# One tile and one transfer for four pairs of heads, and another layout for stored queries, keys and projection operands

## Chip, cores and metric

The kernel runs on 1 core of one Trainium2 chip. The metric is the device time of one execution in microseconds (us), taken as the median of several executions. The engines are TensorE (PE, with its weight loads PEld), VectorE (DVE), ScalarE (ACT), GpSimd (POOL) and SyncE (SP), whose queue issues nearly all transfers (DMAs).

## The reference, cut to what matters

One layer of a hybrid backbone over 1,024 latent tokens and 256 context tokens, width 1,024, fp32. One input projection feeds 8 heads of differential attention and 16 recurrent heads (RWKV-7, width 64, forwards and backwards); both outputs are gated and go through one output projection.

```python
u = h @ lp['w_in']
q, k, v, g_a, u_b, g_b = jnp.split(u, [...], axis=-1)
...
s = jnp.einsum('bqhmd,bkhmd->bhmqk', qblk, k).astype(F32) * scale   # m: the two halves of a head
p = jax.nn.softmax(s, axis=-1)
a = p[:, :, 0] - lam * p[:, :, 1]
...
sa = jnp.einsum('bhvk,bhk->bhv', S, -kk_t)                          # one recurrent step
S = S * w_t[:, :, None, :] + sa[..., None] * b_t[:, :, None, :] + v_t[..., None] * k_t[:, :, None, :]
y = jnp.einsum('bhvk,bhk->bhv', S, r_t)
...
x = x + gate[:, None, :] * (jnp.concatenate([o_a, o_b], axis=-1) @ lp['w_out'])
```

## The kernel before, in words

The program has two stages. All instructions are written out, and a scheduler puts them in order per engine by its own model and by priorities; each engine then runs its instructions strictly in that order.

**First stage** (`chunk`, `plan`, the generators `b_*`): for 66 blocks of 128 columns of `w_in`, three products of 24 matmuls each (`psg`, four PSUM banks) over 512, 512 and 256 tokens. A generator of each block does the rest between the products of later blocks. Weights `w` have one buffer and are loaded one block ahead; ACT casts them to `whi`, DVE and POOL make `wlo`. `b_k` prepares the recurrence of one pair of heads: `operands` and `gram` make the tiles `ra` (two buffers), `bk` and `km` (one each) for 8 chunks of 32 tokens and store them to the DRAM scratch `ra`, `kt` and `bt`. `b_qk` rotates a head's queries or keys (`suq`, `suk` are copies with swapped rows, made by DMA) and splits them into a high part `hi` and a low part. For the first six heads the high part goes in pieces of 512, 512 and 256 tokens through one buffer (tag `hi`, L624 to L627): ACT casts a piece, DVE subtracts, SP stores it, and the next cast writes the same buffer. Cached keys go through it too (`ko`, `ch`, L598 to L609), and their low part is `ck`. The low part of a whole head is one store (L628). For the last two heads the high part is one tile and one store. Scratch `qhi`, `qlo`, `khi`, `klo` has rows of 128 per head, so each store is `128 x n`.

**Second stage** (`mix_phase`): 10 items (2 groups of four pairs x 5 segments of 256 tokens), 4 parts per item, 2 steps per part, 80 steps in sequence. A step works for four pairs; these stand in two duos `w`, each with its own tiles `L` and `R` (two slots each, for even and odd parts). `step` multiplies `R` by `L` three times: L933 (into `bank[0]`, copied back into `R` by ACT, L940), L951 (into `bank[1]`, multiplied by the decay into the next `R` by DVE, L962) and L975 (the output `y`). `prep` (L812) multiplies `Bt` by the inverse `Tb` for one duo of the next part at the end of each step, and `put` (L818) copies that into `L`. `load_part` (L770 to L786) loads `L` from `kt` and `ra` and `R` from `vb`; `load_early` (L792 to L803) loads `Bt` and `Tb`. `inverse` makes the 32x32 inverses on POOL, in the layout `td0`. Between a step's pieces `fill` issues attention (`load_q`, `load_k`, `scores` L1099, `values` L1144), layer norms and the output projection (`project`, operand tile `of` from the scratch `oT`), each in its own order.

Of the kernel before, what the change touches and what calls it, by code (L numbers as in the profile page):

```python
# [10 lines left out]
F32 = mybir.dt.float32  # L11
# [7 lines left out]
P = 128  # L19
# [64 lines left out]
def tile_kernel(ctx: ExitStack, tc: tile.TileContext, i: dict, o: dict, heads=H, phases=3):  # L84
# [15 lines left out]
    scratch("ra", [H // 2, 5, NF, HD, 2, 2, 2, HN * HD])  # L100
    scratch("kt", [H // 2, 5, NF, CH, 2, 2, 2, HN * P])
    scratch("bt", [H // 2, 5, NF, 2, 2, CH, 2, HN * P])
# [21 lines left out]
    with ExitStack() as p1:  # L124
# [321 lines left out]
        def gram(p, d, it, c0, ra, bk):  # L446
# [13 lines left out]
            for h in range(2):  # L460
                nc.sync.dma_start(s["kt"][p // 2, it, :, :, p % 2, h, d].rearrange("f r y -> r f y"),
                                  km[64 * h:64 * h + CH].rearrange("r (f c) x -> r f (c x)", f=NF))
                nc.sync.dma_start(s["bt"][p // 2, it, :, h, d, :, p % 2].rearrange("f r y -> r f y"),
                                  km[64 * h + CH:64 * h + 64].rearrange("r (f c) x -> r f (c x)", f=NF))

        def operands(p, d, r, k, kn, wx, td, ta, c0):
# [12 lines left out]
            for h in range(2):  # L479
                nc.sync.dma_start(s["ra"][p // 2, it, :, :, p % 2, h, d].rearrange("f r y -> r f y"),  # L480
                                  ra[64 * h:64 * h + 64].rearrange("r (f c) x -> r f (c x)", f=NF))
# [96 lines left out]
        def b_qk(which, h):  # L578
            rows = slice(h * P, (h + 1) * P)
# [13 lines left out]
            if which == "k":  # L593
# [14 lines left out]
                nc.sync.dma_start(s["khi"][rows, 0:PAST], ch)  # L608
                nc.sync.dma_start(s["klo"][rows, 0:PAST], cv)  # L609
# [3 lines left out]
            if h >= heads - 2:  # L613
# [6 lines left out]
                spill(s[which + "hi"][rows, off:off + T], hi)  # L620
                spill(s[which + "lo"][rows, off:off + T], u[:, 0:T])
                return
            for n0, n in CHUNKS:
# [3 lines left out]
                spill(s[which + "hi"][rows, off + n0:off + n0 + n], hi)  # L627
            spill(s[which + "lo"][rows, off:off + T], u[:, 0:T])  # L628
# [96 lines left out]
def inverse(nc, s, td, rows, aw, tt, tmp):  # L725
    n = 32 * len(rows)
    for g, (p, sg) in enumerate(rows):
        bt = s["bt"][p // 2, sg + 1, :, :, :, :, p % 2].rearrange("f h d t y -> (f h d) t y")
        for c in range(HN):
            nc.sync.dma_start(aw[32 * g + c:32 * g + 32:HN], bt[:, :, c * P + 96:c * P + P])  # L730
# [14 lines left out]
def mix_phase(ctx, tc, i, o, s, ident, nhalf, dram, td0, neglam, subg, lnh, heads, psm):  # L745
# [8 lines left out]
    for w in duos:  # L754
        for n in range(2):
            L = cp.tile([P, 2, 2, 2, HN, P], F32, name=f"L{w}{n}")
            R = cp.tile([P, HN, 2, 2, P], F32, name=f"R{w}{n}")
            for e in range(2):
                for h in range(2):
                    for d in range(2):  # L760
                        nc.vector.tensor_copy(L[0:64, e, h, d, :, 0:64],
                                              ident[0:64, 0:64].unsqueeze(1).broadcast_to([HD, HN, HD]))
            slots[w, n] = (L, R)

# [5 lines left out]
    def load_part(j):  # L770
        m, f = j // NF, j % NF
        p0, sg = items[m]
        for w in duos:
# [4 lines left out]
        for w in duos:  # L778
            p = p0 + 2 * w
            L, R = slots[w, j % 2]  # L780
            for d in range(2):
                t0 = tok0(sg, d) + CH * HN * (NF - 1 - f if d else f)
                src = s["vb"][t0:t0 + CH * HN, p * P:(p + 2) * P].rearrange("(c t) y -> t c y", t=CH)
                nc.sync.dma_start(R[64:96, :, d].rearrange("t c e v -> t c (e v)"), src[:, ::-1] if d else src)
            nc.sync.dma_start(L[0:64, :, :, :, :, 64:128].rearrange("r e h d c y -> r e (h d c) y"),
                              s["ra"][p // 2, sg + 1, f].rearrange("r e h d (c y) -> r (e h d c) y", y=HD))  # L786
# [5 lines left out]
    def load_early(j, w):  # L792
        m, f = j // NF, j % NF
        p0, sg = items[m]
        p = p0 + 2 * w
        Bt = cp.tile([P, 2, HN, P], F32, tag=f"Bt{w}", name=f"Bt{j}_{w}")
        nc.sync.dma_start(Bt.rearrange("r e c y -> r (e c y)"),
                          s["bt"][p // 2, sg + 1, f].rearrange("h d r e y -> (h d) r (e y)"))
        Tb = cp.tile([P, 2, HN, CH], F32, tag=f"Tb{w}", name=f"Tb{j}_{w}")
# [3 lines left out]
        early[j, w] = (Bt, Tb)  # L803

    def prep(j, w, pp, chain):
        Bt, Tb = early.pop((j, w))
        for e in range(2):
            for c in range(HN):
                for q in range(4):
                    n = 96 * (HN * e + c)  # L810
                    g = slice(32 * q, 32 * q + 32)
                    follow(nc.tensor.matmul(pp[g, n:n + 96], Tb[g, e, c, :], Bt[g, e, c, 0:96], start=True, stop=True,  # L812
                                            tile_position=(32 * q, 32 * q)), chain)

    def put(j, w, pp):
        L = slots[w, j % 2][0]
        for q in range(4):
            nc.scalar.copy(L[96:128, :, q // 2, q % 2, :, 0:96],  # L818
# [7 lines left out]
    for w in duos:  # L826
        load_early(0, w)
# [8 lines left out]
    for w in duos:  # L836
        load_early(1, w)
# [44 lines left out]
    def start_item(w, m):  # L882
        p0, sg = items[m]
        R = slots[w, 0][1]
# [725 lines left out]
```

## Time and profile before

| | us |
|---|---|
| median of 3 runs | 2551.7 (2549.16 to 2551.72) |
| profiled execution, its own time | 2542.46 |
| its span, first to last instruction | 2540.3 |
| PE busy | 2299.6 (91%) |
| DVE / ACT / POOL busy | 1491.8 / 1222.8 / 1149.4 |
| mean granted clock of PE | 0.954 of full |

A line of the chain of waits gives the start and the time of a piece of work that the end of the program waited for; a DMA there counts from its issue to its landing. A line of the order in time gives start, busy time, engine and line, output and input, and in brackets how long the engine was idle before and what ended that. A DMA's own line (SPq) is only its issue.

### The profile page before, as it was taken

What the parts mean: (1) busy time and instruction counts of PE and PEld (TensorE: products, weight loads), DVE (VectorE), ACT (ScalarE), POOL (GpSimd) and SP (SyncE); (2) the same over time, 40 slices, a digit from 0 to 9 for tenths busy, and PEclk for the clock granted to TensorE, in tenths of its full rate; (3) what the DMA queues carried; (4) which work ended last, traced back from release to release, by engine and by line L of the source; (5) the groups of instructions that cost most, each with busy time, mean ns of one, the idle gap of its engine ahead of it and who ended that gap; (6) DMA issues with size and microseconds to landing.
All of it is one profiled execution on the core that took longest, in us unless ns stands there. A gap on an engine that the chain in (4) does not pass through costs nothing.

```text
span 2540.3 us, 60748 instructions
## 1 busy us (share of the span) xinstructions
PE 2299.6 (91%) x23907; PEld 1880.0 (74%) x23907; DVE 1491.8 (59%) x2950; ACT 1222.8 (48%) x2528; POOL 1149.4 (45%) x1665
## 2 busy tenths in 40 slices
PE   5999999999999999999578887999898889897886
PEld 4888888888888888887467676767686677675675
DVE  5665574646555755433347675666665564666676
ACT  3333444343433444332366676667566565553353
POOL 4244244352433443447554764457485121133274
PEclk9999999999999999999689898999999899998998
DMA  7455656566655565665998897786879889767435
GB/s 246 111 153 135 185 146 171 142 167 164 156 138 160 144 162 138 163 168 158 240 183 166 188 188 167 160 181 148 191 176 224 221 205 223 178 182 217 141 122 183
DMA packets 544893, 437.59 MB, mean 172 GB/s; under 512 B 182151, under 2 KB 481331, under 8 KB 542048
## 3 DMA queue, kind: packets, MB, share of 16 engines
q1 hardware_dynamic: 542512, 427.96, 66.8%
q0 software_dynamic: 2096, 5.75, 1.2%
q8 instruction: 189, 3.10, 0.5%
q14 instruction: 96, 0.79, 0.1%
HBM read 258.69 MB, written 163.86 MB: 166 GB/s over the span
## 4 chain that ended last, share of the span: by engine, by line
PE 53%; DMA 14%; POOL 9%; DVE 8%; SPq 6%; ACT 5%; issue 4%; POOLq 0%; DVEq 0%; ACTq 0%
PE sc L1099 4%; PE po L1144 4%; PE pg L452 3%; PE bank L951 3%; PE pa L1129 2%; PE yb L812 2%; DMA yn<-y 1%; PE pso L1352 1%; PE ptk L456 1%; PE bank L975 1%; PE bank L933 1%; PE psg_v L338 1%; ACT pb L1107 1%; PE psg_v L339 1%; PE psg_v L337 1%
## 5 line engine op out<-in xcount | busy, mean ns | idle before, releaser
L1099 PE MATMUL sc<-ka,q 128*128 128x512 f32 (+1 forms) x832 | 296.0, 447 | 40.1 <-DVE pb L1102 34.3
L1107 ACT ACTIVATE pb<-pb,mn 128x1536 f32<-128x1536 f32 (+1 forms) x160 | 218.3, 1365 | 97.8 <-DVE pb L1102 94.7
L1102 DVE TENSOR_SCALAR_CACHE_REDUCE pb<-sc,mn 128x512 f32<-128x512 f32 x256 | 191.5, 748 | 113.1 <-PE sc L1099 104.8
L1144 PE MATMUL po<-vk,aT 128*128 128x128 f32 x1600 | 233.6, 287 | 3.7 <-ACT aT L1131 3.6
L1144 PEld LDWEIGHTS po<-vk,aT 128*128 128x128 f32 x1600 | 212.9, 198 | 22.7 <-ACT aT L1131 5.7
L484 POOL TENSOR_SCALAR ta<-ta,ka 128x256 f32<-128x256 f32 x80 | 93.8, 1172 | 291.3 <-DVE bk L482 287.0
L738 POOL TENSOR_TENSOR tmp<-aw,tt 128x31 f32<-128x31 f32 (+15 forms) x310 | 165.5, 534 | 120.3 <-DMA aw<-bt 40.0
L459 ACT COPY km<-ptk 64x256 f32<-64x256 f32 x320 | 117.6, 367 | 209.5 <-PE ptk L456 169.8
L1099 PEld LDWEIGHTS sc<-ka,q 128*128 128x128 f32 x832 | 142.1, 202 | 81.7 <-DVE pb L1102 53.1
L740 POOL TENSOR_TENSOR tt<-tt,tmp 128x31 f32<-128x31 f32 (+15 forms) x310 | 183.3, 591 | 19.9
L962 DVE TENSOR_TENSOR R<-bank,wc 64x256 f32<-64x256 f32 x312 | 131.0, 420 | 76.4 <-PE bank L951 73.0
L818 ACT COPY L<-yb 32x384 f32<-32x384 f32 x312 | 146.6, 470 | 56.6 <-PE yb L812 52.8
L453 DVE TENSOR_TENSOR km<-pg,msk 128x512 f32<-128x512 f32 x80 | 55.2, 690 | 200.2 <-PE pg L452 188.4
L1121 DVE SCALAR_TENSOR_TENSOR pb<-pb,cc,pb 128x512 f32<-128x512 f32 (+1 forms) x208 | 170.6, 867 | 2.0
L1102 DVE TENSOR_SCALAR_CACHE_REDUCE pb<-sc 128x512 f32<-128x512 f32 (+1 forms) x160 | 101.3, 635 | 87.0 <-PE sc L1099 72.8
L1129 PE MATMUL pa<-ident,pb 128*128 128x128 f32 x800 | 135.1, 287 | 14.1 <-DVE acc L1346 9.0
L1131 ACT COPY aT<-pa 128x512 f32<-128x512 f32 (+1 forms) x208 | 115.1, 570 | 64.4 <-PE pa L1129 62.3
L940 ACT COPY R<-bank 32x256 f32<-32x256 f32 x320 | 116.1, 363 | 54.1 <-PE bank L933 49.9
L951 PEld LDWEIGHTS bank<-R,L 128*64 128x64 f32 x2560 | 91.9, 150 | 56.4 <-ACT R L940 36.1
L951 PE MATMUL bank<-R,L 128*64 128x64 f32 x2560 | 105.0, 239 | 29.3 <-ACT R L940 29.0
L1129 PEld LDWEIGHTS pa<-ident,pb 128*128 128x128 f32 x800 | 97.9, 145 | 43.6 <-DVE acc L1346 11.6
L1336 POOL TENSOR_TENSOR olo<-of,ohi 128x512 fp32r<-128x512 f32 x30 | 39.0, 1298 | 195.6 <-ACT ohi L1335 120.9
(354 smaller groups left out, 6388.2 us busy)
## 6 DMA issues: line engine op xcount, KB each, us to landing
acc<-acc SPq DMA_DIRECT2D x50, 512.0 KB
ra<-ra SPq DMA_DIRECT2D x160, 128.0 KB
kt<-km SPq DMA_DIRECT2D x160, 128.0 KB
bt<-km SPq DMA_DIRECT2D x160, 128.0 KB
Bt<-bt SPq DMA_DIRECT2D x80, 256.0 KB
L<-kt SPq DMA_DIRECT2D x80, 256.0 KB
L<-ra SPq DMA_DIRECT2D x80, 256.0 KB
R<-vb SPq DMA_DIRECT2D x160, 64.0 KB
```

The source lines that it names most:

```text
L459: nc.scalar.copy(km[64 * h:64 * h + 64, e:NC:2, 0:HD], pt[64 * e:64 * e + 64, :, 64 * h:64 * h + 64])
L738: e.tensor_tensor(mv, aw[:n, t, t + 1:CH].unsqueeze(2).broadcast_to([n, w, j]), tt[:n, t:t + 1, 0:j].broadcast_to([n, w, j]), op=ALU.mult)
L740: e.tensor_tensor(tt[:n, t + 1:CH, 0:j], tt[:n, t + 1:CH, 0:j], mv, op=ALU.add)
L818: nc.scalar.copy(L[96:128, :, q // 2, q % 2, :, 0:96], pp[32 * q:32 * q + 32, 0:192 * HN].rearrange("p (e c y) -> p e c y", e=2, y=96))
L951: x = nc.tensor.matmul(bank[1][hv(h), o_:o_ + 64], L[:, e, h, d, k, 0:64], R[:, k, d, e, hv(h)], start=True, stop=True, tile_position=(0, ...
L962: hold(nc.vector.tensor_tensor(dst[:, :, :, hv(h)], bank[1][hv(h), 256 * w:256 * w + 256].rearrange("p (d e v) -> p d e v", e=2, d=2), wcs ...
L1099: nc.tensor.matmul(sc, q[:, v, m, qc], ka[:, m, 0:kn], start=(v == 0), stop=(v == 1))
L1102: nc.vector.tensor_scalar(pm[:, c * 512:c * 512 + kn], sc, -0.125, mn[:, c - 1:c] if c else None, op0=ALU.mult, op1=ALU.min, accum_out=mn[ ...
L1107: soon.append(lambda: nc.scalar.activation(v, v, AF.Exp, bias=mn[:, c:c + 1], scale=-1.0, accum_out=B["l"][:, m, B["b"]:B["b"] + 1]))
L1121: nc.vector.scalar_tensor_tensor(a, B["p"][1][:, v], B["cc"], a, op0=ALU.mult, op1=ALU.add)
L1129: nc.tensor.transpose(pt[:, t * P:(t + 1) * P], B["p"][0][:, 512 * c + t * P:512 * c + (t + 1) * P], ident)
L1144: nc.tensor.matmul(po, B["aT"][c][:, t * P:(t + 1) * P], vk[:, t, :], start=(c == 0 and t == 0), stop=(c == last and t == nt - 1))
```

## The change

Scratch for queries becomes `[head, row, part, half, token]`, for keys `[head, part, row, half, token]`, so that high and low part load in one transfer. The scratch `ra`, `kt`, `bt` holds four pairs together (`NL` = 4). In the second stage one `L`, `R`, `Bt` and `Tb` serve four pairs: one load of `kt`, `ra` and `Bt`, two of `vb` and one of `Tb` per part. The lanes of the inverses are renumbered (pair innermost) to match. DVE's product with the decay covers four pairs at once. `prep` and `put` of the second duo come after the first products of the second step, before ACT's copies, and `load_early` follows them once per part. The scratch `oT` is put in the order in which the projection reads its rows.

```diff
-    scratch("qhi", [D, T])
-    scratch("qlo", [D, T])
-    scratch("khi", [D, NK])
-    scratch("klo", [D, NK])
+    scratch("q", [H, HD, 2, 2, T])
+    scratch("k", [H, 2, HD, 2, NK])
...
         def b_qk(which, h):
-            rows = slice(h * P, (h + 1) * P)
+            dq = lambda v, c: (s["q"][h, :, v, :, c] if which == "q" else s["k"][h, v, :, :, c]).rearrange("r m t -> m r t")
...
-                nc.sync.dma_start(s["khi"][rows, 0:PAST], ch)
-                nc.sync.dma_start(s["klo"][rows, 0:PAST], cv)
+                nc.sync.dma_start(dq(0, slice(0, PAST)), ch)
+                nc.sync.dma_start(dq(1, slice(0, PAST)), cv)
...
-                spill(s[which + "hi"][rows, off + n0:off + n0 + n], hi)
-            spill(s[which + "lo"][rows, off:off + T], u[:, 0:T])
+                spill(dq(0, slice(off + n0, off + n0 + n)), hi)
+            spill(dq(1, slice(off, off + T)), u[:, 0:T])
...
-        for w in duos:
-            p = p0 + 2 * w
-            L, R = slots[w, j % 2]
-            nc.sync.dma_start(L[64:96].rearrange("r e h d c y -> r (e h d c y)"),
-                              s["kt"][p // 2, sg + 1, f].rearrange("r e h d y -> r (e h d y)"))
+        L, R = slots[j % 2]
+        nc.sync.dma_start(L[64:96].rearrange("r x h d c y -> r (x h d c y)"),
+                          s["kt"][p0 // NL, sg + 1, f].rearrange("r x h d y -> r (x h d y)"))
...
-        src = tds[m].rearrange("t (x f q u) s -> f q t x (u s)", x=NL, f=NF, q=4)
-        for e in range(2):
-            nc.sync.dma_start(Tb[:, e].rearrange("t u s -> t (u s)"), src[f, :, :, 2 * w + e])
+        src = tds[m].rearrange("t (f q u) s -> f q t (u s)", f=NF, q=4)
+        nc.sync.dma_start(Tb.rearrange("t c x s -> t (c x s)"), src[f])
...
+            if k == HN - 1 and j + 1 < n_part:
+                prep(j + 1, 1, yb, chain)
...
+        if k == HN - 1 and j + 1 < n_part:
+            put(j + 1, 1, yb)
+            if j + 2 < n_part:
+                load_early(j + 2)
...
-            if j + 1 < n_part:
-                prep(j + 1, k, yb, chain)
+            if k == 0 and j + 1 < n_part:
+                prep(j + 1, 0, yb, chain)
...
-        for v, w in enumerate(("qhi", "qlo")):
-            src = s[w][h * P:(h + 1) * P, n0:n0 + n].rearrange("(m r) t -> r m t", m=2)
-            for e in range(2):
-                nc.sync.dma_start(q[64 * e:64 * e + 64, v], src)
+        for e in range(2):
+            nc.sync.dma_start(q[64 * e:64 * e + 64].rearrange("r v m t -> r (v m) t"),
+                              s["q"][h, :, :, :, n0:n0 + n].rearrange("r v m t -> r (v m) t"))
...
-        for e, w in enumerate(("khi", "klo")):
-            nc.sync.dma_start(ka[64 * e:64 * e + 64],
-                              s[w][h * P:(h + 1) * P, k0:k0 + n].rearrange("(m r) k -> r m k", m=2))
+        nc.sync.dma_start(ka, s["k"][h, :, :, :, k0:k0 + n].rearrange("e r m k -> (e r) m k"))
...
-            for b in range(2):
-                r = D * b + sl[0]
-                nc.sync.dma_start(of[:, na * b:na * b + na], s["oT"][r:r + na * P, cols].rearrange("(k p) t -> p k t", p=P))
+            nc.sync.dma_start(of[:, 0:KS], s["oT"][4 * j * P:4 * j * P + KS * P, cols].rearrange("(k p) t -> p k t", p=P))
```

SyncE's order in the first stage, at the stores of the third head's queries (`hiq`, `uq` are the high and low part), before:

```order
L379 DMA qhi<-hiq_0_5747 128x512
L379 DMA gb<-gb_5346 128x1280
L379 DMA bv<-s_v_5248 128x1280
L161 DMA w_av_5786<-w_in 128x8x128
L379 DMA qhi<-hiq_512_5751 128x512
L461 DMA kt<-km_5533 32x4x256
...
L480 DMA ra<-ra_5644 64x4x128 x2
L379 DMA qhi<-hiq_1024_5755 128x256
L379 DMA qlo<-uq_5212 128x1280
L585 DMA suk_5829<-uk_5585 16x1024 x6
```

The same place of the change:

```order
L377 DMA q<-hiq_0_5745 2x64x512
L377 DMA bv<-s_v_5246 128x1280
L377 DMA gb<-gb_5344 128x1280
L159 DMA w_av_5784<-w_in 128x8x128
L377 DMA q<-hiq_512_5749 2x64x512
L459 DMA kt<-km_5531 32x4x256
...
L478 DMA ra<-ra_5642 64x4x128 x2
L377 DMA q<-hiq_1024_5753 2x64x256
L377 DMA q<-uq_5210 2x64x1280
L583 DMA suk_5827<-uk_5583 16x1024 x5
```

The stores keep their places; the shape of their DRAM side (the last word of a row) is 2x64xn in place of 128xn. The tile side still has 128 rows.

PE's order in the second stage, the second step of a part (`sc`, `pa` and `po` are attention, `yb` the prepared operand of the next part), before:

```order
L933 MATMUL bank_12451<-R_11747,L_11746 32x64 x2
L1099 MATMUL sc_4_0_0_13303<-ka_0_12462,q_1_12491 128x512 x2
...
L951 MATMUL bank_12452<-R_11727,L_11726 64x64 x8
L951 MATMUL bank_12452<-R_11747,L_11746 64x64 x8
L975 MATMUL bank_12451<-R_11727,L_11726 32x64 x8
L975 MATMUL bank_12451<-R_11747,L_11746 32x64 x8
L812 MATMUL yb<-Bt_1_13381,Tb_1_13383 32x96 x16
```

The same step of the change:

```order
L920 MATMUL bank_12425<-R_11733,L_11732 32x64 x16
L801 MATMUL yb<-Bt_13926,Tb_13928 32x96 x16
L1084 MATMUL sc_7_1_2_13955<-ka_2_12438,q_1_12460 128x512 x2
...
L941 MATMUL bank_12426<-R_11733,L_11732 64x64 x16
L964 MATMUL bank_12425<-R_11733,L_11732 32x64 x16
```

The 16 products of the second duo (`yb`) moved from the end of the step to behind its first products.

## Rows read from the trace of the kernel before

**Rows 1.** The page, busy us (share of the span) and instructions of an engine.

```profile
PE 2299.6 (91%) x23907; PEld 1880.0 (74%) x23907; DVE 1491.8 (59%) x2950; ACT 1222.8 (48%) x2528; POOL 1149.4 (45%) x1665
```

**Rows 2.** Stretches: us, PE, PEld, DVE, ACT, POOL busy, clock, DMA share, GB/s.

```profile
60.00:1180.00 1120.00, 1102.44 (x8471) 934.16 (x8470) 630.19 (x942) 431.21 (x818) 471.30 (x518) 1.00 0.59 154
1180.00:1300.00 120.00, 80.23 (x980) 65.16 (x978) 45.75 (x112) 36.38 (x75) 57.46 (x99) 0.76 0.89 196
1300.00:2240.00 940.00, 838.31 (x12613) 660.82 (x12614) 584.81 (x1400) 612.66 (x1350) 449.77 (x823) 0.94 0.81 185
2240.00:2540.00 300.00, 244.89 (x1233) 194.58 (x1231) 200.54 (x434) 120.87 (x249) 144.96 (x183) 0.92 0.54 172
```

**Rows 3.** The chain of waits, third head's keys: start us, us, what.

```profile
574.63 2.88 DMA khi<-ch
577.59 0.63 ACT hik L625
578.24 2.23 DMA khi<-hik
```

**Rows 4.** ACT in order of time, the same place.

```profile
577.59 0.62 ACT L625 CAST hik<-uk 128x512 fp32r<-128x512 f32 x1 [4.05 <-DMA khi<-ch]
...
584.99 0.59 ACT L348 COPY uv<-psg_av 128x512 f32<-128x512 f32 x1
```

**Rows 5.** The tile hik: its engines' idle time before it, us and times, until.

```profile
  DMA khi<-ch: 20.4, 6
  DMA khi<-hik: 15.3, 8
```

**Rows 6.** The page's packets, and DMA issues by line, count and KB each.

```profile
DMA packets 544893, 437.59 MB, mean 172 GB/s; under 512 B 182151, under 2 KB 481331, under 8 KB 542048
...
L<-ra SPq DMA_DIRECT2D x80, 256.0 KB
...
aw<-bt SPq DMA_DIRECT2D x80, 64.0 KB
...
Tb<-td SPq DMA_DIRECT2D x160, 32.0 KB
...
n<-kk SPq DMA_DIRECT2D x16, 5.0 KB
```

**Rows 7.** Stretches, columns as in rows 2: a start-up load and a burst of stores.

```profile
25.00:35.00 10.00, 5.81 (x205) 4.56 (x205) 2.74 (x8) 1.75 (x3) 1.47 (x2) 1.00 1.07 374
...
535.00:555.00 20.00, 18.90 (x154) 16.09 (x153) 9.15 (x15) 7.18 (x16) 10.02 (x14) 1.00 0.87 248
```

**Rows 8.** SyncE's queue in order of time: the third head's query stores.

```profile
535.16 0.35 SPq L379 DMA_DIRECT2D qhi<-hiq  x1
...
544.87 0.57 SPq L379 DMA_DIRECT2D qhi<-hiq  x1
```

**Rows 9.** SyncE's queue: issues of Bt and Tb for one duo.

```profile
1263.71 0.34 SPq L797 DMA_DIRECT2D Bt<-bt  x1
1264.13 1.15 SPq L802 DMA_DIRECT2D Tb<-td  x2
```

**Rows 10.** The page's chain that ended last, by engine.

```profile
PE 53%; DMA 14%; POOL 9%; DVE 8%; SPq 6%; ACT 5%; issue 4%; POOLq 0%; DVEq 0%; ACTq 0%
```

**Rows 11.** The page's groups L962, L453; the tile R: first products, first and last start.

```profile
L962 DVE TENSOR_TENSOR R<-bank,wc 64x256 f32<-64x256 f32 x312 | 131.0, 420 | 76.4 <-PE bank L951 73.0
...
L453 DVE TENSOR_TENSOR km<-pg,msk 128x512 f32<-128x512 f32 x80 | 55.2, 690 | 200.2 <-PE pg L452 188.4
...
L933 PE MATMUL bank<-R,L x2560: 216/219/317, 1227.1 to 2233.2; 96*32 96x64 f32 x197
```

**Rows 12.** The tile Tb: its engine's idle time, us and times, until.

```profile
  DMA Tb<-td: 21.7, 11
```

**Rows 13.** The chain of waits: two of PE's products pg in a burst.

```profile
538.40 1.15 PE pg L452 x32
...
546.30 1.08 PE pg L452 x32
```

More of the change, by code (lines that the diff above doesn't have):

```diff
@@ L619, in b_qk @@
                 yield
-                spill(s[which + "hi"][rows, off:off + T], hi)
-                spill(s[which + "lo"][rows, off:off + T], u[:, 0:T])
+                spill(dq(0, slice(off, off + T)), hi)
+                spill(dq(1, slice(off, off + T)), u[:, 0:T])
                 return
@@ L753, in mix_phase @@
     slots = {}
-    for w in duos:
-        for n in range(2):
-            L = cp.tile([P, 2, 2, 2, HN, P], F32, name=f"L{w}{n}")
-            R = cp.tile([P, HN, 2, 2, P], F32, name=f"R{w}{n}")
-            for e in range(2):
[L759 to L763, printed above, removed]
+    for n in range(2):
+        L = cp.tile([P, NL, 2, 2, HN, P], F32, name=f"L{n}")
+        R = cp.tile([P, HN, 2, NL, P], F32, name=f"R{n}")
+        for x in range(NL):
+            for h in range(2):
+                for d in range(2):
+                    nc.vector.tensor_copy(L[0:64, x, h, d, :, 0:64], ident[0:64, 0:64].unsqueeze(1).broadcast_to([HD, HN, HD]))
+        slots[n] = (L, R)
     def tok0(sg, d):
@@ L824, in follow @@
         chain.append(x.ins.name)
-    for w in duos:
-        load_early(0, w)
+    load_early(0)
     for j in range(2):
@@ L835, in mix_phase @@
         put(0, w, pp)
-    for w in duos:
-        load_early(1, w)
+    load_early(1)
     yield True
@@ L944, in step @@
         with ahead(HPC):
[L945 to L963 removed]
+            for x_ in range(NL):
+                for d in range(2):
+                    for h in range(2):
+                        o_ = 256 * d + 64 * x_
+                        x = nc.tensor.matmul(bank[1][hv(h), o_:o_ + 64], L[:, x_, h, d, k, 0:64],
+                                             R[:, k, d, x_, hv(h)], start=True, stop=True, tile_position=(0, 64 * h))
+                        held(x, chain)
+            if k < HN - 1:
+                dst = R[0:64, k + 1]
+            elif f == NF - 1 and sg == 3:
+                dst = None
+            else:
+                dst = slots[(j + 1) % 2][1][0:64, 0]
+            for h in range(2):
+                if dst is not None:
+                    hold(nc.vector.tensor_tensor(dst[:, :, :, hv(h)], bank[1][hv(h), :].rearrange("p (d x v) -> p d x v", d=2, x=NL),
+                                                 wcs[p0][hv(h), :, sg + 1, :, c:c + 1].rearrange("p x d o -> p d x o").broadcast_to([HD, 2, NL, HD]),
+                                                 op=ALU.mult))
         g = c // HN
@@ L967, in step @@
         with ahead(HPY):
-            for w in duos:
-                L, R = slots[w, j % 2]
-                for e in range(2):
-                    o_ = 256 + P * w + 64 * e
-                    for h in range(2):
-                        for d in range(2):
-                            q = 64 * d + 32 * h
-                            x = nc.tensor.matmul(bank[0][q:q + 32, o_:o_ + 64], L[:, e, h, d, k, 64:96], R[:, k, d, e, hv(h)],
-                                                 start=True, stop=True, tile_position=(0, q))
-                            follow(x, chain)
-            if j + 1 < n_part:
-                prep(j + 1, k, yb, chain)
+            for x_ in range(NL):
+                o_ = 256 + 64 * x_
+                for h in range(2):
+                    for d in range(2):
+                        q = 64 * d + 32 * h
+                        x = nc.tensor.matmul(bank[0][q:q + 32, o_:o_ + 64], L[:, x_, h, d, k, 64:96], R[:, k, d, x_, hv(h)],
+                                             start=True, stop=True, tile_position=(0, q))
+                        follow(x, chain)
+            if k == 0 and j + 1 < n_part:
+                prep(j + 1, 0, yb, chain)
             nc.scalar.copy(ysb[m, g][:, k], bank[0][:, 256:512].rearrange("p (x v) -> p x v", x=NL))
-        if j + 1 < n_part:
-            put(j + 1, k, yb)
-        if j + 2 < n_part:
-            load_early(j + 2, k)
+        if k == 0 and j + 1 < n_part:
+            put(j + 1, 0, yb)
         fill(1)
@@ L1311, in project @@
         na = len(sl)
[L1312 removed]
+        need_a = [r // P for r in sl]
+        sl = sl[:na - 1] + [D + r for r in sl] + sl[na - 1:]
         KS = len(sl)
@@ L1321, in project @@
             cols = slice(t * P, t * P + P)
-            while not ({("b", j, t)} | {("a", r // P, t) for r in sl[:na]} <= done):
+            while not ({("b", j, t)} | {("a", h, t) for h in need_a} <= done):
                 yield
```

100 lines of the change are left out of this document (36 added, 64 removed).

## The prediction

> **What bounds the kernel now.** I read the page's busy table first, then the stretches, then single stores. TensorE (PE) is busy 91% of the span and ScalarE (ACT) 48% [rows 1]. By stretches, PE is busy 1102.44 of 1120 us from 60 to 1180 us, which is the projection stage; 80 of 120 in the turn to the second stage; 838 of 940 in the recurrence and attention; 245 of 300 in the last products [rows 2]. So the first stage has some 18 us of PE idle time, the later ones 197 us (40 + 102 + 55), and a change can give something back only in the later ones. In the first it can only take. What it would take there is buffers: the chain of waits runs through stores of queries and keys although ACT is busy only 431 of 1120 us. In the burst at 574 us, the store khi<-ch (2.88 us) and then khi<-hik (2.23 us) lie on the chain, with a cast into the same buffer between them [rows 3]; ACT stands idle for 4.05 us before the first of these casts, and the copies that empty PE's banks (uv is one) stand behind the casts in its order [rows 4]. Over the run hik's casts waited 20.4 us in 6 places for ch's store and 15.3 us in 8 for their own [rows 5].
>
> **What the change does to the stores.** In the first stage the order of the engines stays nearly as it was (the piece of SyncE's order shown above is the pattern); what alters is the shape of 72 stores, whose DRAM side now begins with a dimension of 2 where it had 128 rows. If a transfer is dealt out to the 16 DMA engines by its first dimensions, these 72 run on two of them. The trace shows that dealing for a first dimension of 4. The page counts 182,151 packets under 512 B [rows 6]. Carried by transfers are aw 80 x 512, L<-ra 80 x 1024 and Tb 160 x 128 such pieces (143,360; the piece sizes follow from the shapes) and some 4,400 small ones (states, vectors, POOL's own). That leaves some 34,400, which I read as the marks that each engine sets at the end of its part. At 16 marks for each of SyncE's 2,282 transfers (counted along its queue) they would be 36,512; the difference, 2,112, is 176 x 12, and exactly 176 transfers, 160 of Tb and 16 of n [rows 6], have a DRAM side that begins with 4. So I take it that the 72 stores use two engines.
>
> The Trainium skill ("DMA: Bandwidth & Descriptors", section "Why a DMA increments its semaphore by 16 and not by 1") says that a DMA uses the largest number of engines up to 16 that divides the first dimension above 1 of both sides; by it these stores get two. By that rule the trace agrees, with the 2,112 missing marks.
>
> *Price of one store.* An engine moves 23.4 GB/s at best (374 GB/s from 25 to 35 us, all 16 busy) and 17.8 in a burst of this stage (248 / (0.87 x 16)) [rows 7]. A 256 KB store is 16 KB for each of 16 engines (0.7 to 0.9 us) and 128 KB for each of two (5.6 to 7.4): 4.9 to 6.4 us more. A 640 KB store of the low part is 12.3 to 16.1 us more. I take the low end, since the long rows that these stores write are like those of the 374 GB/s stretch. Per head the stores are 1,280 KB of queries and 1,792 KB of keys, so two engines carry 59 to 77 us more per head, 471 to 618 in all. They are busy 0.59 of 1120 us already (661) [rows 2], so they would have 1132 to 1279 us of work in a stage of 1120: they are about full.
>
> *What of it is on the path.* In the keys' burst the first cast waits for ch's store (+4.9); ck's store stands between it and hik's on the same two engines (+4.9); the second cast waits for hik's first store (+4.9), the third for its second (+4.9): 19.6 us in ACT's order, with the copies that free PE's banks behind it. In the queries' burst two such waits make 9.8 us; today the first and the third of the three stores go out at 535.16 and 544.87 us [rows 8]. That is 29.4 us per head for six heads, 176 us; the last two heads split into one large tile, so only the next item is theirs. The low part follows (12.3 us on the two engines), and everything stored or loaded after it, kt, bt, ra, suk and the weights in the rows that follow, is complete only when its share on these two engines is. Buffers are short there (one km, one bk, two ra, weights one step ahead). I count half of it: 16 x 12.3 / 2 = 98. Off goes what today's waits do not cost: the stores are on the chain in only some bursts, so I take 2.5 us in each of 12 bursts, about the present length of a store [rows 3], 30 us. First stage: 176 + 98 - 30 = **+244 us**. Bounds: 117 (casts alone, with 5 us of slack in each burst) and 425 (high price: 6 x 38.6 = 232, and three quarters of the backlog, 193).
>
> **The second half.** Per part 14 issues become 6 (kt, R, ra, Bt and Tb for four pairs at once), 320 fewer over 40 parts; queries 48, keys 32 and projection operands 40 fewer make 440 of 2,282. An issue takes 0.34 us (Bt) to 0.58 (Tb, 1.15 for two) [rows 9]; at some 0.5 us each it is 220 us less in SyncE's queue. Most of that queue runs ahead of need: it holds 6% of the chain, 152 us [rows 10], and 440 / 2,282 of that is 29 us. The bytes are the same. On VectorE (DVE) 312 products of 64x256 at 0.42 us become 156 of twice the columns; the nearest row with 512 columns takes 0.69 [rows 11], so 131 - 108 = 23 us less of an engine that is busy 585 of 940; I count 4 us on the path. Against this, Bt and Tb have one buffer for both duos and are loaded after the second duo's products of the step before, so they have about one step to arrive where each duo had two. A step is 12.7 us (80 steps start from 1227.1 to 2233.2 us, [rows 11]); PE has waited 21.7 us in 11 places for Tb [rows 12]; I add 8. In PE's order the second duo's products now stand behind the first products of the step, where PE would wait for ACT's copies anyway; nothing. L and R setup, inverse lanes (the same 80 loads with rows in another order) and the output layout oT: nothing, their counts and sizes stay. Sum of the second half: -29 - 4 + 8 = **-25**, bounds -100 (half of the later idle time) and +40 (the waits for Tb three times what they are).
>
> **Sum.** 2542.46 + 244 - 25 = 2761 us against the profiled execution (span 2540.3); the median of the runs shown is 9.2 us above it, so 2551.7 + 219 = **2771 us**.
>
> **The rivals.**
> *Forecast, 0.80*: two engines, and the waits land on the path as walked: 2609 (+117, and 60 gained in the second half) to 2952 (+425 and 25).
> *Only the capacity counts, 0.10*: two engines, but the buffers and ACT's idle time take up each burst, and only the surplus of 1132 to 1279 us over 1120 is paid: +12 to +159, with -25 some 2539 to 2686, in the middle 2610. For it: ACT, DVE and POOL are busy under 60% of the stage. Against: the chain already passes through these stores when they take 2 to 3 us [rows 3].
> *Faster, 0.10*: the stores cost nothing on the path, because they are spread wider after all or because the casts' waits fall into time in which PE has other work, and the 440 issues are gained: 2551.7 - 25 = 2527, at best 2450. It decides if one burst delays ACT by less than PE can run ahead of it: PE's products of pg come some 8 us apart (538.40 and 546.30 us, [rows 13]) and need ACT's and DVE's km, of which there is one, so PE has 8 to 10 us; my walk has 9.8 in the queries' burst and 19.6 in the keys'. The Trainium skill ("DMA: Bandwidth & Descriptors", section "Rules for kernel authors") speaks for this rival: coalesce many small transfers into a large one. Here Tb's 32 KB transfers, 160 of them, are the only such ones that matter, and they sit in the queue, not on PE.
>
> **How the numbers follow.** A measurement of this kernel can tell about 0.2%, 5 us, from no change. The forecast lies wholly above; of the capacity case 0.07 is slower, 0.02 the same and 0.01 faster; of the third 0.09 is faster and 0.01 the same. So slower 0.87, same 0.03, faster 0.10. The range leaves out the third case and some ends of the others: 2610 to 2955.
>
> **What would show it.** Right: the stretch to the end of the projections is 120 to 430 us longer with PE busy well under 98% of it; rows of a store k<-ch or k<-hik on the chain take 7 us and more; ACT's hik casts wait over 100 us in sum; the second half keeps its length or is slightly shorter, with 440 fewer issues and DVE's product at 0.65 to 0.75 us. Wrong: if those stores still land in 2 to 3 us, the premise is; if they land in 7 and the first stage is as long as before, the walk is; if the second half alone moves by over 60 us, its terms are.

## The result and the profile after

The changed kernel takes **2880.14 us** (median of 4 runs, 2874.8 to 2882.18) against 2550.43 us (4 runs beside it): a ratio of **1.1293 [1.1271, 1.1315]**, 330 us slower. The forecast was 2771 us, in a range of 2610 to 2955, with a chance of 0.87 for slower.

The page after, beside [rows 1], [rows 6] and [rows 10]:

```profile
PE 2398.6 (83%) x23907; PEld 1931.7 (67%) x23907; DVE 1437.0 (50%) x2794; ACT 1219.6 (42%) x2528; POOL 1132.2 (39%) x1665
...
DMA packets 511399, 437.51 MB, mean 152 GB/s; under 512 B 155063, under 2 KB 449123, under 8 KB 509840
...
PE 42%; DMA 28%; DVE 7%; POOL 6%; SPq 6%; ACT 5%; issue 5%; POOLq 0%; DVEq 0%; ACTq 0%
```

The bytes are the same, the transfers' share of the chain has doubled from 14 to 28%. The stretches after (columns as in [rows 2]; the first reaches to the end of the projections):

```profile
60.00:1480.00 1420.00, 1162.53 (x8491) 977.68 (x8489) 609.55 (x942) 426.28 (x817) 466.64 (x531) 0.91 0.47 122
1480.00:1600.00 120.00, 64.32 (x779) 51.63 (x780) 35.62 (x87) 32.85 (x69) 38.28 (x65) 0.70 0.71 171
1600.00:2580.00 980.00, 895.75 (x12817) 684.49 (x12817) 567.93 (x1270) 619.07 (x1360) 460.00 (x844) 0.93 0.81 182
```

For nearly the same products (8,491 where 8,471 stood) the projections need 1420 us instead of 1120. Of these 300, PE's idle time is 240: 1420 - 1162.53 = 257 where [rows 2] give 1120 - 1102.44 = 18. The other 60 are products that take longer at a granted clock of 0.91 where it was 1.00.

The tile `bank`, after: the first products of the recurrence, with first and last start (the row beside the last one of [rows 11]):

```profile
L920 PE MATMUL bank<-R,L x2560: 216/219/317, 1543.4 to 2567.4; 96*32 96x64 f32 x197
```

The recurrence begins at 1543.4 where it began at 1227.1 us (+316), runs 1024.0 where it ran 1006.1 us (+18), and 311.4 us follow the start of its last step where 307.1 did (+4). So the loss lies in the first stage and the turn behind it. There, one burst of keys on the chain of waits, as in [rows 3] (start us, us, what):

```profile
894.48 7.97 DMA k<-ch
...
902.53 0.62 ACT hik L623
...
903.17 9.54 DMA k<-hik
...
913.43 7.95 DMA k<-hik
...
922.50 18.77 DMA k<-uk
```

The stores that took 2.88 and 2.23 us take 8 to 9.5, and the low part of the head 18.77. The tiles `hik` and `hiq` after, what their engine waited for (us, times), beside [rows 5]:

```profile
  DMA k<-hik: 94.6, 12
  DMA k<-ch: 48.9, 6
...
  DMA q<-hiq: 81.7, 12
```

In sum 225 us, where `hik` waited 15.3 + 20.4 and `hiq` 9.4: 180 us more. The stores that stand behind these in the queue are late too. The tile `km` (one buffer), after; before, no wait for this store is among its rows:

```profile
  DMA bt<-km: 194.9, 19
```

PE itself waits at the products of the recurrence's operands (the same stretch of the projections, what waited for what, us, times, longest; before, 14.7 us):

```profile
PE pg L450 <- POOL bk L484: 93.7, 24, 17.0
```

In the second half SyncE's queue has 1,842 transfers where it had 2,282, the 440 fewer of the forecast. DVE's product and the waits for `Tb`, beside [rows 11] and [rows 12]:

```profile
L952 DVE TENSOR_TENSOR R<-bank,wc 64x512 f32<-64x512 f32 x156 | 107.0, 686 | 62.4 <-PE bank L941 61.2
...
  DMA Tb<-td: 33.6, 6
```

### The profile page after: what moved, and what is told of

Its sections match the earlier page's. It is cut to its first block, busy times and chain, and to the rows that moved or that the text cites. A ratio compares the mean times of both kernels' runs of the same rounds, so it can differ in the third digit from the quotient of the medians.

```text
span 2878.8 us, 59956 instructions
## 1 busy us (share of the span) xinstructions
PE 2398.6 (83%) x23907; PEld 1931.7 (67%) x23907; DVE 1437.0 (50%) x2794; ACT 1219.6 (42%) x2528; POOL 1132.2 (39%) x1665
## 4 chain that ended last, share of the span: by engine, by line
PE 42%; DMA 28%; DVE 7%; POOL 6%; SPq 6%; ACT 5%; issue 5%; POOLq 0%; DVEq 0%; ACTq 0%
PE sc L1084 4%; PE po L1129 4%; DMA k<-hik 3%; PE yb L801 3%; PE bank L941 2%; PE pa L1114 2%; DMA wst<-w_out 2%; DMA Tb<-td 2%; DMA bt<-km 2%; DMA acc<-acc 2%; PE pg L450 2%; DMA q<-hiq 2%; DMA k<-ch 2%; PE pso L1337 2%; PE pso L1338 2%
## 5 line engine op out<-in xcount | busy, mean ns | idle before, releaser
L1129 PE MATMUL po<-vk,aT 128*128 128x128 f32 x1600 | 242.9, 290 | 14.2 <-ACT aT L1116 10.2
L450 PE MATMUL pg<-ra,bk 64*64 64x64 f32 x2560 | 101.6, 235 | 113.9 <-POOL bk L484 93.7
L450 PEld LDWEIGHTS pg<-ra,bk 64*64 64x64 f32 x2560 | 90.1, 147 | 138.4 <-POOL bk L484 102.5
L952 DVE TENSOR_TENSOR R<-bank,wc 64x512 f32<-64x512 f32 x156 | 107.0, 686 | 62.4 <-PE bank L941 61.2
L801 PE MATMUL yb<-Bt,Tb 32*32 32x96 f32 x2496 | 108.7, 262 | 31.6 <-DMA Tb<-td 24.3
```

The lines of the kernel that those rows point to most:

```text
L450: nc.tensor.matmul(pg[hs, c, :], bk[hs, c, :], ra[hs, c, :], start=True, stop=True)
L801: follow(nc.tensor.matmul(pp[g, n:n + 96], Tb[g, c, 2 * w + e, :], Bt[g, 2 * w + e, c, 0:96], start=True, stop=True, tile_position=(32 * q ...
L1129: nc.tensor.matmul(po, B["aT"][c][:, t * P:(t + 1) * P], vk[:, t, :], start=(c == 0 and t == 0), stop=(c == last and t == nt - 1))
```

## The experiments

In all of them the time is the median, the ratio is that to the kernel before on the same chip, and "start" and "length" are the first start of the recurrence's first products and the time to their last, from the row of the tile `bank`. "Stretches" counts, in PE's order, the unbroken rows of products into `bank` or `yb`, nearly all the recurrence's own small ones (in every kernel 23 of the rows are projection products behind it); "yb" is PE's busy time in `yb<-Bt,Tb`, 2,496 in the trace, which has two records for each of these fp32 products (x16 in PE's order is 32 there). The last two columns are used from e9 on.

| kernel | us | ratio | start | length | stretches | yb us |
|---|---|---|---|---|---|---|
| before | 2544 to 2550 | 1 | 1227.1 | 1006.1 | 352 | 94.2 |
| the change | 2880.1 | 1.1293 | 1543.4 | 1024.0 | 455 | 108.7 |
| e1, stores in halves | 2580.8 | 1.0135 [1.0093, 1.0177] | 1245.1 | 1034.1 | 455 | 109.3 |
| e2, before with two-engine stores | 2866.4 | 1.1255 [1.1215, 1.1294] | 1545.6 | 1008.7 | 353 | 94.4 |
| e3, early loads per duo | 2630.2 | 1.0293 [1.0227, 1.0358] | 1252.9 | 1063.3 | 456 | 126.3 |
| e4, Tb in quarters | 2573.4 | 1.0108 [1.0073, 1.0143] | 1246.8 | 1023.4 | 434 | 115.7 |
| e5, queries and keys alone | 2544.3 | 0.9978 [0.9953, 1.0002] | 1247.1 | 980.4 | 362 | 86.8 |
| e6, second half alone | 2531.7 | 0.9933 [0.9904, 0.9961] | 1234.8 | 985.3 | 366 | 98.6 |
| e7, e6 with four products | 2552.5 | 1.0015 [0.9991, 1.0040] | 1235.1 | 1002.2 | 355 | 94.5 |
| e8, products moved alone | 2536.3 | 0.9960 [0.9931, 0.9989] | 1232.7 | 991.7 | 417 | 97.3 |
| e9, e6 and queries, plain stores | 2566.6 | 1.0071 [1.0045, 1.0098] | 1226.9 | 1035.2 | 464 | 113.4 |
| e10, e6 and keys | 2546.4 | 0.9989 [0.9969, 1.0010] | 1241.1 | 1000.4 | 405 | 101.8 |
| e11, e6 and Tb in quarters | 2578.3 | 1.0128 [1.0095, 1.0161] | 1231.1 | 1032.2 | 482 | 124.5 |
| e12, e9 with yb unbroken | **2496.5** | **0.9815 [0.9785, 0.9844]** | 1228.1 | **956.9** | 276 | 71.7 |

**The stores, e1 and e2.** e1 is the change with each store of queries or keys issued as two, one for each half of 64 rows, so that no side begins with 2:

```diff
+            def store(v, c, t):
+                for m in range(2):
+                    nc.sync.dma_start(dq(v, c)[m], t[64 * m:64 * m + 64])
...
-                nc.sync.dma_start(dq(0, slice(0, PAST)), ch)
...
+                store(0, slice(0, PAST), ch)
```

> The change, with each of the 72 stores of queries and keys issued as two, one per half of 64 rows; layout and everything else stay. Theory A (the stores are slow because their DRAM side begins with 2 and so they use two of the 16 DMA engines): the first stage ends near 1234 us again, as before the change, in place of 1538; the total is 2540 to 2590 us, what is left over 2550 being the second stage. Rival B (the new layout itself is slow to write, because the rows of a store lie 14 to 20 KB apart): the stage stays near 1538 us and the total near 2880.

e2 is the kernel before, with a spare row after each half of a head in the scratch, so that the two halves no longer merge into 128 rows; nothing else of the change is in it:

```diff
-    scratch("khi", [D, NK])
+    scratch("khi", [H, 2, HD + 1, NK])
...
-                nc.sync.dma_start(s["khi"][rows, 0:PAST], ch)
+                nc.sync.dma_start(s["khi"][h, :, 0:HD, 0:PAST], ch)
```

> The kernel before, with one edit: the scratch of queries and keys has a spare row after each half of 64, so that the stores' DRAM side begins with 2 (rows still 5 or 7 KB apart); loads, transfers and tiles as before. Theory A: the first stage ends near 1538 us and the total is 2830 to 2890 us. Rival B: no change, 2545 to 2560.

e1 gives back 299 of the 330 us, and e2 loses 319 without any other part of the change. The page of e2 shows the engines by a count:

```profile
DMA packets 543885, 437.59 MB, mean 153 GB/s; under 512 B 181143, under 2 KB 480323, under 8 KB 541040
```

It has 1,008 packets fewer than [rows 6], all of them under 512 B, and 1,008 is 72 x 14: each of the 72 stores lacks the marks of 14 engines. The change's own trace has the same: two marks for each of these stores, four for each of 56 transfers that begin with 4 (40 of Tb, 16 of n) and 16 for the other 1,714 make 27,792, which is the number of 4-byte packets in SyncE's queue there. With that the rule of the Trainium skill that the prediction quoted ("DMA: Bandwidth & Descriptors", section "Why a DMA increments its semaphore by 16 and not by 1") is borne out to the packet. What its casts waited for is what they waited for in the change (tile `hik` of e2):

```profile
  DMA khi<-hik: 94.2, 12
  DMA khi<-ch: 49.8, 6
```

and with the stores in halves the projections run as before (e1, the stretch of the first row of [rows 2]):

```profile
60.00:1180.00 1120.00, 1088.32 (x8367) 920.50 (x8366) 617.26 (x937) 424.88 (x810) 446.36 (x506) 0.99 0.60 151
```

PE's idle time falls to 32 us and its clock is back at 0.99, so the 60 us of longer products go with the waits. The Trainium skill ("DMA: Bandwidth & Descriptors", section "Rules for kernel authors") says of two transfers to disjoint partition halves not to bother. Here e1's halves are the faster by 299 us, since the one store that they replace has 2 as its first dimension.

**The second half, e3 to e8.** e1 is still some 33 us above the kernel before, where the sum of the second half was -25. e3 is e1 with one `Bt` and `Tb` for each duo again, loaded at each step's end as before the change, which also puts the second duo's products back there; e4 is e1 with each load of `Tb` as four of 32 rows.

```diff
-        Tb = cp.tile([P, HN, NL, CH], F32, tag="Tb", name=f"Tb{j}")
+        Tb = cp.tile([P, HN, 2, CH], F32, tag=f"Tb{w}", name=f"Tb{j}_{w}")
...
-            if k == 0 and j + 1 < n_part:
-                prep(j + 1, 0, yb, chain)
+            if j + 1 < n_part:
+                prep(j + 1, k, yb, chain)
```

```diff
-        nc.sync.dma_start(Tb.rearrange("t c x s -> t (c x s)"), src[f])
+        for q in range(4):
+            nc.sync.dma_start(Tb[32 * q:32 * q + 32].rearrange("t c x s -> t (c x s)"), src[f, q])
```

> e1_halves, with Bt and Tb in two tiles again (one per duo), each loaded at the end of its own step and multiplied at the end of the next but one, as before the change: 160 issues more in the second stage. Theory C (the second stage of the change is some 30 us longer because Bt and Tb have one step to arrive where they had two): 20 to 40 us faster than e1_halves. Rival D (it is longer only because its start is disturbed by the late stores of the first stage): e1_halves is already at 2540 or below and this is no faster, or slower by the issues, 0 to 15 us.

> e1_halves, with the load of Tb issued as four, one per 32 rows, so that its DRAM side begins with 32 in place of 4: 120 issues more. Theory E (Tb is late because 128 KB go through four DMA engines): 15 to 30 us faster than e1_halves, and waits for Tb mostly gone. Theory C (lead time): the gain is under 10 us. Rival D: no faster, or slower by the issues.

e3 waited less for `Tb` (18.8 us where e1 waited 33.2) and was 49 us slower than e1 all the same, which neither theory had. e4 gave 7 us, and its interval overlaps that of e1. So the waits for `Tb` are not what is lost; the price of the lead time alone stays open, since e3 also undid the move of the products. Then the parts alone: e5 is the kernel before with the new scratch and one-piece loads of queries and keys (stores in halves), e6 the change without that part, e7 is e6 with DVE's product as four of 256 columns in a step, and e8 is the kernel before with the second duo's `prep` and `put` moved behind the first products, as in the change. The loads of the keys in e5 against the kernel before (e6 is the same turned round, against the change):

```diff
-        for e, w in enumerate(("khi", "klo")):
-            nc.sync.dma_start(ka[64 * e:64 * e + 64],
-                              s[w][h * P:(h + 1) * P, k0:k0 + n].rearrange("(m r) k -> r m k", m=2))
+        nc.sync.dma_start(ka, s["k"][h, :, :, :, k0:k0 + n].rearrange("e r m k -> (e r) m k"))
```

e7 against e6:

```diff
-            for h in range(2):
-                if dst is not None:
-                    hold(nc.vector.tensor_tensor(dst[:, :, :, hv(h)], bank[1][hv(h), :].rearrange("p (d x v) -> p d x v", d=2, x=NL),
+            for w in duos:
+                for h in range(2):
+                    if dst is not None:
+                        xs_ = slice(2 * w, 2 * w + 2)
+                        hold(nc.vector.tensor_tensor(dst[:, :, xs_, hv(h)], bank[1][hv(h), :].rearrange("p (d x v) -> p d x v", d=2, x=NL)[:, :, xs_],
```

e8 against the kernel before, the place behind the first products (the one at the step's end keeps the first duo's):

```diff
+            if k == HN - 1 and j + 1 < n_part:
+                prep(j + 1, 1, yb, chain)
```

> The kernel before with the queries' and keys' part alone: new scratch layout, loads in one piece (80 issues fewer), stores as two halves (72 more). e1_halves is 1.35% above before: its first stage ends 16 us later and its recurrence takes 27 us longer. Theory F (the halves cost the first stage): the first stage ends 10 to 20 us later than before, the recurrence takes 1005 to 1015 us, total 2555 to 2570. Rival G (nothing of it comes from this part): 2540 to 2552.

> The change without the queries' and keys' part (scratch, stores and loads of these as before). Theory F: the first stage ends near 1234 us as before, and what is left is the second stage: 2560 to 2580, recurrence 1025 to 1040 us. Rival G: the first stage ends near 1250 here too. If my sum for the second stage were right (-25 us), the total would be 2520 to 2530.

> e6_no_qk, with VectorE's product with the decay as four of 64x256 per step as before in place of two of 64x512. Theory H (the larger product delays VectorE's other work, so that attention waits): 10 to 25 us faster than e6_no_qk. Rival: slower by 5 to 25 us (two products of 0.69 us against four of 0.42, once per step on the recurrence's path).

> The kernel before, with one edit: the second duo's products for the next part, their copies into L and its loads of Bt and Tb move behind the first products of the second step, as in the change. Theory I (the moved products stand on the recurrence's path and lengthen it): 15 to 35 us slower than before. Rival J (they fill a wait of TensorE for ScalarE's copies): 0 to 30 us faster, as e3_early_per_duo was 49 us slower than e1_halves.

The second half alone is **17 us faster** than before, near the forecast's -25. e7 loses 21 of these again. Its DVE row, beside that of the change above:

```profile
L956 DVE TENSOR_TENSOR R<-bank,wc 64x256 f32<-64x256 f32 x312 | 131.0, 420 | 54.1 <-PE bank L943 50.7
```

Four products of 0.42 us in a row end 1.68 us after the first starts, two of 0.69 after 1.37. That is 0.31 us a step, 24 us over 78 steps, if the last one is what PE waits for, and 21 were measured. But the traces do not show that path. The median step is as long in e6 as in e7 (11.24 and 11.25 us), and in both PE starts the next step's first product some 2 us after the last of DVE's (median 2.23 and 1.96 us). The 17 us by which e7's recurrence is longer are what is left of steps that differ by up to 9 us either way. And e5, which has four products in a step, has a shorter recurrence (980.4) than e6 with two (985.3). So the price of the larger product stays open, and the 21 us agree with the sum by luck as far as is known. e8 is 10 to 12 us faster than the kernel before (3 to 18 by its interval). But e5 (-4) and e6 (-17) together make e1 (+33): some 54 us come from neither part.

**The parts together, e9 to e12.** e9 is e6 with the queries alone, in a scratch `[head, part, half, row, token]`, whose stores are 128 x n again and whose loads merge as in the change; e10 is e6 with the keys alone, as in e1; e11 is e6 with the edit of e4. The queries' scratch and load in e9:

```diff
-    scratch("qhi", [D, T])
-    scratch("qlo", [D, T])
+    scratch("q", [H, 2, 2, HD, T])
...
+                              s["q"][h, :, :, :, n0:n0 + n].rearrange("v m r t -> r (v m) t"))
```

> The second-half change without the q/k part (2532, first stage 1240, recurrence 990) plus the queries alone, in a scratch [head, part, half, row, token]: every query store is again 128 x n as before the change, and a group of queries loads in two transfers in place of four; keys stay as before the change. Theory K (the load merge is harmless, and the trouble of the q/k part lies in its stores and in the keys): first stage 1235 to 1245, recurrence 980 to 995, in all 2520 to 2538, the best so far. Theory L (merging the query loads and the recurrence's loads hurt one another, because the scheduler's order of the second stage changes with every removed issue): recurrence 1010 or more, in all 2550 or more.

> The second-half change plus the keys part alone, stored in halves and loaded in one piece; queries as before the change. The whole change with half stores took 2581 (first stage 1250, recurrence 1038), without the q/k part 2532 (1240, 990). If the keys carry the 49 us: 2565 or more, with a recurrence over 1020. If the queries carry it: 2545 or less, with a first stage of 1245 to 1250 and a recurrence under 1000. If each carries a share (an order that is worse by chance): between the two.

> The second-half change without the q/k part, with each load of the inverses Tb as four transfers of 32 rows in place of one whose outer side is 4. With the q/k part this edit gave 7 us. If the single load's late landing (12 us on the chain) is what it saves: 2517 to 2527. If the seven were the order's noise: 2527 to 2540.

The queries cost 35 us on top of e6, the keys 15, and e11's edit 47, outside both of its ranges, where beside the queries and keys it had gained 7, not clear of the noise. An edit that is worth so different a time is not the only thing that is being measured. What differs as well is the order of PE: the scheduler puts attention and projection products between the recurrence's small ones, and with each change of the instructions it does so in other places. In e9, one set of `yb` products, as PE has them:

```
L803 MATMUL yb<-Bt_21637,Tb_21639 32x96 x7
L1341 MATMUL pso_4_0_20938<-wohi_19338,ohi_4_20768 128x512
L803 MATMUL yb<-Bt_21637,Tb_21639 32x96
L1342 MATMUL pso_4_0_20938<-wolo_19339,ohi_4_20768 128x512
L803 MATMUL yb<-Bt_21637,Tb_21639 32x96
L1343 MATMUL pso_4_0_20938<-wohi_19338,olo_4_20769 128x512
```

e12 is e9 with a higher priority for these products, and nothing else:

```diff
     def prep(j, w, pp, chain):
+        with tc.high_priority(offset=1000):
+            prep_(j, w, pp, chain)
+
+    def prep_(j, w, pp, chain):
         Bt, Tb = early[j]
```

> The slow mixture (queries merged with plain stores, plus the second half: 2566.6, recurrence 1040) with the products yb<-Bt,Tb alone given a higher priority, so that the scheduler no longer puts attention products between them. In the order of PE the products of the recurrence (bank and yb) then stand in 276 unbroken stretches, where that mixture had 464, the second half without the q/k part 366, and the whole change with half stores 455. Theory M (the 35 to 50 us that the parts lose together are torn series: 32-row products that run four abreast only when they stand together, yb busy 110.6 us for 2416 products in the slow mixture against 96.8 for 2432 in the fast one, and a chain that is held up by what stands between): recurrence 985 to 1005, yb busy under 95, in all 2515 to 2535. Theory N (tearing is only a companion of an order that is late for other reasons, such as waits for Tb or attention put off to the end): 2555 or more. Between the two, tearing is a part of it.

The same set then stands in two whole rows (here the first; the second follows the next step's first products):

```
L970 MATMUL bank_12426<-R_11734,L_11733 32x64 x16
L807 MATMUL yb<-Bt_21637,Tb_21639 32x96 x16
L1345 MATMUL pso_4_0_20938<-wohi_19338,ohi_4_20768 128x512
```

e12 takes 2496.5 us, 70 less than e9 and 35 less than e6 (65 and 30 by the ratios, since e12 ran on another chip) and **1.85% less than the kernel before**, which is more than theory M had. PE's products `yb`, by line, columns as in [rows 11], in e9:

```profile
L803 PE MATMUL yb<-Bt,Tb 32*32 32x96 f32 x2496 | 113.4, 260 | 31.2 <-DMA Tb<-td 22.6 <-issue 4.1 <-DMA R<-vb 2.9
```

and in e12:

```profile
L807 PE MATMUL yb<-Bt,Tb 32*32 32x96 f32 x2496 | 71.7, 253 | 29.7 <-DMA Tb<-td 21.3 <-DMA R<-vb 2.9 <-ACT L L813 2.7
```

One product lasts as long as before (260 and 253 ns) and the waits for `Tb` are the same, but PE is busy with them for 113.4 / 2496 = 45 ns each in e9 and 29 ns in e12: they overlap one another when they stand together. The first products of the steps gain too: PE is busy 78.4 us with them in e9 and 65.0 in e12.

Where the time goes can be read by items (ten, of eight steps each). In the first four items `yb` stands in whole sets in e9 as well; in the last six it stands in 161 rows where e12 has 46. The first four items and the last six, of e9 (columns as in [rows 2]):

```profile
1226.90:1593.60 366.70, 302.96 (x5222) 247.40 (x5222) 219.37 (x496) 250.24 (x550) 232.60 (x431) 0.90 0.90 193
1593.60:2267.10 673.50, 639.23 (x8115) 465.81 (x8115) 362.21 (x806) 388.89 (x852) 259.06 (x465) 0.91 0.76 175
```

and of e12:

```profile
1228.10:1590.60 362.50, 299.38 (x5226) 244.02 (x5228) 220.33 (x496) 250.43 (x550) 233.28 (x428) 0.90 0.90 195
1590.60:2189.70 599.10, 544.09 (x8128) 434.30 (x8127) 360.52 (x810) 385.13 (x853) 262.96 (x466) 0.95 0.86 197
```

Where the sets are whole in both, 4 us lie between them; where e9's are torn, 74, with 95 us more of PE's time for as many products, 42 of it in `yb`. There is no fixed price for a tear. In the seventh and ninth items PE is busy 7 us longer in e9, and the items take only 0.5 and 1.2 us longer, since idle time makes up for it. The fifth and eighth take 21 and 25 us longer, and in them the granted clock is 0.84 and 0.89 where e12 has 0.95 and 1.00. How much of the 74 us is the clock, and whether the tears lowered it, is not shown. Nor does e12 separate whole sets from early ones: a higher priority can also move the products ahead.

The Trainium skill ("TensorEngine Tiling (Array Packing)", section "Tiling Modes") says that products on different tiles run in parallel, and that a change of the tiling mode drains TensorE. The 45 and 29 ns agree with that; what a single such drain costs, no run here shows.

Across the table the length goes with the stretches, but not strictly: 362 and 366 go with 980 and 985 us, 405 with 1000, 434 to 482 with 1023 to 1063, 276 with 957. Against it, the kernel before, e2 and e7 have 352 to 355 stretches and take 1002 to 1009 us, and e8 has 417 and takes 992. These stay open; four DVE products in a step are no reason, since e5 has them too. PE's time in `yb` goes with the length more closely (87 to 99 us with 980 to 1009, 102 to 126 with 1000 to 1063), which tells where the time lies and not what made it.

## Why the prediction was right, and where it was not

**Premise and place: right.** The 72 stores run on two engines (e2's 1,008 missing marks; the 34,400 marks that the prediction reached by subtraction are the count of 4-byte packets in SyncE's queue to the packet), they are the loss (e1, e2), and they act where the walk put them: the casts wait for the stores, the stores stand on the chain. The rival in which only the engines' capacity counts is out: it ended at +159 for the first stage, which lost 300 (316 to the start of the recurrence). So is the faster one: the point that it named was a burst of more than 8 to 10 us, and e2's casts waited 144 us for six heads' keys, 24 us a burst.

**First stage, +244, measured +300: right in mechanism, too small.** The casts: I had 29.4 us a head, 176; they waited 180 more, so the walk holds. Inside it two sizes offset one another. A store took 5.1 to 5.7 us more (7.97 less 2.88, 7.95 less 2.23) where I had 4.9, and `ck`'s store made `hik`'s first piece only 1.6 us longer than the second, where I had 4.9 again. So the keys' casts waited 18 us more a head and not 19.6, the queries' 12 and not 9.8. The sum of 244 meets PE's added idle time of 240, but how the casts (176), the low part (98) and the slack taken off (30) share it can't be read: the waits lie on different engines and overlap. The backlog that the low part stood for is there, in `km`'s 195 us, and PE's idle time ended mostly at the recurrence's operands `bk` and `km` (179 us), and for 38 us at the copies that empty its banks, where the walk had put it. What the sum lacks is a term: PE's products took 60 us longer at a clock of 0.91. [Rows 2] show 1.00 for a stage without pauses and 0.76 in the turn, so rows to suspect it from were there. The turn takes 16 us more on top (316 to the start of the recurrence, and 318 in e2, which has the stores alone).

**Second half, -25: right for that part alone, wrong within the change.** In the change it came to +22 (18 in the recurrence, 4 after it), and beside e2, which has the stores alone, to +10 by the ratios; e1, without the stores' loss, has +33. All lie inside the bounds of -100 to +40 but have the other sign; e6, the part by itself, gives -17, where the -25 was near. Within the sum:
- DVE's larger product, "4 us on the path": e7 gives 21, but no trace shows them on the path of the steps, so the term stays open.
- The moved products, "nothing", are worth 10 to 12 us by e8, in the order which that kernel has.
- The shorter lead time of `Bt` and `Tb`, +8: the waits for `Tb` rose by 12 us (33.6 against 21.7 in [rows 12]). e3 brought no time back, but it undid the move of the products and its order is torn more (yb 126.3 us), so the price alone stays open.
- The issues, -29: not tried by themselves. In e6, with 360 issues fewer, the pieces of SyncE's queue on the chain add up to 137 us where they were 144, only 7 us less, while the transfers' share rose from 14 to 17%.

**The step that failed**, in a forecast whose main part held, is the adding up of the second half, each term priced in the order that PE had before. Its "nothing" behind "In PE's order the second duo's products now stand behind the first products of the step" took the order at one place for the order of the stage; the prediction compared orders in the first stage and at that place alone. Over the second stage the scheduler tore the recurrence's products into 455 stretches in place of 352, which no line of the diff shows; e6, with the moved products and without the queries' and keys' part, has 366. e12 shows what a higher priority of `yb` gives back in the mixture e9: 70 us. That torn sets also make the 54 us of e1, which has 455 stretches, is likely by the table, but e1 was not run with whole sets. Nor were e6 and the kernel before, so what of e12's 1.85% belongs to the change and what the kernel before would gain in the same way stays open.

## What to carry to other kernels

Before a layout is changed for the sake of its loads, look at the first dimension of both sides of its stores: 72 transfers of `2 x 64 x n` were 299 us slower here in sum than 144 of `64 x n`, and a layout of the queries with the same merged load and 128-row stores (e9) costs the first stage nothing. Where a scheduler fills gaps, count how often it breaks up sets of small products before believing what any single edit is worth: the same edit was worth nothing clear of the noise in one order and took 47 us in another, and a higher priority for one kind of set gave more (70 us) than all of the second half's edits by themselves (17). When a sum meets a measured difference, as with DVE's product, look whether the single steps differ by it too.

## What the runs showed of the hardware

A store confined to two engines delays more than itself: in the five bursts of keys that lie on the change's chain, `hik`'s first piece, which follows `ck`'s store in SyncE's queue, took 9.54 to 10.31 us, its second piece 7.79 to 8.02 and `ch`'s store 7.92 to 8.53 (9.53 to 10.75, 7.84 to 7.99 and 7.91 to 8.58 in e2). And the clock adds to waits: 240 us of added idle time came with 60 us of longer products, which went away with the waits (0.91 in the change, 0.99 in e1).
